# Latent attention's queries: channels on partitions for all tokens at once, in a step of three small parts

## Chip, cores and metric

The kernel runs on one core of one Trainium2 chip. The metric is the device time of one execution in microseconds, the median of the runs shown. TensorE (PE in the profile) does all matrix products and the transposes, VectorE (DVE), ScalarE (ACT) and GpSimd (POOL) do the elementwise work, and SyncE (SP) issues nearly all transfers.

## What is computed

Two layers of a network work on 384 tokens: 128 context tokens and 256 latent tokens. Each layer has a mixer of four attention branches (A to D) between one wide input projection and one output projection, and then an MLP. The change lies in branch A, latent attention. Cut to what matters (`wuq` is `mla_w_uq`, 256 x 384):

```python
q_lat, kv_lat, k_pe = h @ w_in            # 256, 128 and 32 columns
qa = (rmsnorm(q_lat, q_norm) @ wuq).reshape(b, t, 4, 96)
q_nope, q_pe = qa[..., :64], qa[..., 64:]  # 64 columns a head without position, 32 with
ckv = rmsnorm(kv_lat, kv_norm)             # also an output, with k_pe
q = concat(q_nope, rope(q_pe))             # rope on the 256 latent tokens only
k = concat(ckv @ w_uk, rope(k_pe) for every head);  v = ckv @ w_uv
o = softmax(q @ k.T * 96 ** -0.5) @ v
```

## The kernel before

The 384 tokens are three tiles of 128. Every large product is made in three passes of a split number (high x high, low x high, high x low): lines L122, L123 and L124, through a helper, so all large products of the program carry these lines. For the weights' halves ScalarE casts the high half (L283) and VectorE subtracts to get the low one (L127). A stream of weight blocks comes over SP's queue.

Inside a layer the program issues *ticks*. A tick is one group of 24 large matmuls (a token tile times eight channel blocks times three passes; 256 columns wide in the projections to the branches, 384 wide in the gates that follow) plus one step of a pipeline, `pipe`. The pipeline holds a list of tasks, each of them a row of stages; every step takes one new task in and runs one stage of every task that is under way. The order of the list is that of the `pipe.add` calls: branch A's preparation, A's attention, C's preparation and attention, D's, then branch B (whose last stages, `out_b`, end in the transposes L1096). A tick also issues some vector steps of a modulation (L378 on VectorE), whose number a tick is set by `TICK_OPS`: none in ticks 1 to 3, one a tick from tick 4, one every second tick from 14, two a tick from 29. Before ticks begin, layer 0 writes the condition's rows, `cond_rows`: four pieces, each a tanh on ScalarE (L233) and two operations on VectorE (L234, L235), into scratch tiles `acc` of the ring `t2`. That ring has ten tiles (`T2N`) and also holds the projections' results: `evac_to` (L644, on ScalarE) copies a PSUM bank out to a `t2` tile, which may have to wait until the tile's earlier user is done. Of the banks for the groups (pool `psg`) a group needs one, so a group has to wait for the copy of the bank that it takes over. A scheduler then orders the instructions of each engine within limits; the order that it makes is what the engines run, each its own from first to last.

Branch A before the change, for each token tile t, in three stages (`prep_a(t)`):

- `norms`: squares and sums on ScalarE (L790, L791), two steps on VectorE (L792, L794), the inverse root as a power on GpSimd (L190); two transposes of the 256 query latents (L799) and their copy (L800); the scaled key latents (L803).
- `up_q`: the product with `wq`, 128 tokens x 384 columns in two parts of 128 channels (L819; each product of full fp32 shows as two matmuls in the trace), transposes of the key latents and of the position key (L821, L822), a copy out on ScalarE that scales by the root (L824), and rotation (`rope`: two multiplications on GpSimd, L765 and L766, beside four operations on VectorE, L768, L771, L772).
- `turn`: four transposes, one a head (L837), and a copy to `qTA` (L838).

Then come `keys_a` (L845 to L847) and `values_a` (L854, L855), and the attention (L690 scores, L728 transposes of the weights, L746 product with the values).

Of the kernel before, what the change touches and what calls it, by code (L numbers as in the profile page):

```python
# [12 lines left out]
AF = mybir.ActivationFunctionType  # L13
ALU = mybir.AluOpType
AX = mybir.AxisListType

P = 128
D = 1024
KT = D // P
NTOK = 384  # L20
L = 2
D_FF = 4096
ALPHA = float((2.0 * L) ** 0.25)
EPS = 1e-6
# [71 lines left out]
def kernel(ctx, tc, a):  # L96
    nc = tc.nc
# [4 lines left out]
    psa = ctx.enter_context(tc.tile_pool(name="psa", bufs=3, space=bass.MemoryType.PSUM))  # L102
# [5 lines left out]
    mm = nc.tensor.matmul  # L108
# [6 lines left out]
    def bank(pool):  # L115
        return pool.tile([P, 512], F32, tag="bank", name=nm("bank"))
# [349 lines left out]
    for l in range(L):  # L466
        last = l == L - 1
        pipe = Pipe()
# [145 lines left out]
        def t2(name):  # L614
            return at.tile([P, 512], F32, tag="t2", name=nm(name), bufs=T2N)
# [163 lines left out]
        va = at.tile([P, 4, 256], F32, tag="va", name=nm("va"))  # L779
        rsa = at.tile([P, 3, 2], F32, tag="rsa", name=nm("rsa"))  # L780

        def prep_a(t):
            st_ = {}
            tok = slice(t * P, (t + 1) * P)
            rs = rsa[:, t]

            def norms():
                x = tm["a", t]
                sq = t2("sq")
                nc.scalar.activation(sq[:, 0:256], x[:, 0:256], AF.Square, accum_out=rs[:, 0:1])  # L790
                nc.scalar.activation(sq[:, 256:384], x[:, 256:384], AF.Square, accum_out=rs[:, 1:2])  # L791
                nc.vector.tensor_scalar(out=rs[:, 0:1], in0=rs[:, 0:1], scalar1=1.0 / 256, scalar2=EPS, op0=ALU.mult,  # L792
                                        op1=ALU.add)
                nc.vector.tensor_scalar(out=rs[:, 1:2], in0=rs[:, 1:2], scalar1=1.0 / 128, scalar2=EPS, op0=ALU.mult,  # L794
                                        op1=ALU.add)
                rsqrt(rs, rs, 2)
                tb = bank(psm)
                for k in range(2):
                    nc.tensor.transpose(tb[:, k * P:(k + 1) * P], x[:, k * P:(k + 1) * P], ident)  # L799
                nc.vector.tensor_copy(sq[:, 0:256], tb[:, 0:256])  # L800
                st_["qlT"] = sq
                kv = x[:, 256:384]
                nc.vector.scalar_tensor_tensor(out=kv, in0=kv, scalar=rs[:, 1:2], in1=rows[:, R_KV:R_KV + P],  # L803
                                               op0=ALU.mult, op1=ALU.mult)
                if t == 0:
                    nc.sync.dma_start(out=a["o_ckv"][0, l], in_=kv)
                    nc.sync.dma_start(out=a["o_kpe"][0, l], in_=x[:, 384:416])
                    st_["pe"] = x[:, 384:416]
                else:
                    r = small([P, 1, 2, 16], "kpe", 2)  # L810
                    rope(r, x[:, 384:416].rearrange("p (h s f) -> p h s f", h=1, s=2), cos_a[:, t - 1, 0:16],
                         sin_a[:, t - 1, 0:16], 16)()
                    st_["pe"] = r.rearrange("p h s f -> p (h s f)")

            def up_q():
                qlT = st_["qlT"]
                qb = bank(psa)
                for k in range(2):
                    mm(qb[:, :384], lhsT=qlT[:, k * P:(k + 1) * P], rhs=wq[:, k], start=(k == 0), stop=(k == 1))  # L819
                tb = bank(psm)  # L820
                nc.tensor.transpose(tb[:, 0:P], tm["a", t][:, 256:384], ident)  # L821
                nc.tensor.transpose(tb[:32, P:2 * P], st_["pe"], ident)  # L822
                q = t2("qA")
                nc.scalar.mul(q[:, :384], qb[:, :384], rs[:, 0:1])  # L824
                nc.vector.tensor_copy(ckvT[:, tok], tb[:, 0:P])
                nc.scalar.copy(kTA[64:96, :, tok], tb[0:32, P:2 * P].unsqueeze(1).to_broadcast([32, 4, P]))
                if t:
                    qv = q[:, :384].rearrange("p (h d) -> p h d", h=4)[:, :, 64:96].rearrange("p h (s f) -> p h s f", s=2)
                    rq = small([P, 4, 2, 16], "rqo", 1)
                    rope(rq, qv, cos_a[:, t - 1, 0:16], sin_a[:, t - 1, 0:16], 16)()  # L830
                    nc.vector.tensor_copy(qv, rq)
                st_["q"] = q

            def turn():
                tb = bank(psm)
                for h in range(4):
                    nc.tensor.transpose(tb[:96, h * P:(h + 1) * P], st_["q"][:, h * 96:(h + 1) * 96], ident)  # L837
                nc.scalar.copy(qTA[:96, :, tok], tb[:96].rearrange("p (h n) -> p h n", h=4))  # L838

            return norms, up_q, turn  # L840

        def keys_a():
            for i in range(2):
# [260 lines left out]


        for t in range(3):
            pipe.add(*prep_a(t))
        pipe.add(keys_a)
        pipe.add(values_a)
        ba, bc, bd = attend(0, lambda g, j, q: qTA[:96, 2 * g + j, q], lambda g, j, k: kTA[:96, 2 * g + j, k],  # L1110
                            lambda g, j, b: va[:, b, (2 * g + j) * 64:(2 * g + j + 1) * 64], MLA_SCALE), \
            attend_cd("c"), attend_cd("d")
# [510 lines left out]
def _pack(v):  # L1623
# [34 lines left out]
    rows[:, R_SINK:R_SINK + 4] = v["win_sink"][:, order]  # L1658
    out["rows"] = rows
    wm = np.zeros((L, P, 1280), f)  # L1660
    wm[:, :, 0:768] = v["mla_w_uq"].reshape(L, 2, P, 384).transpose(0, 2, 1, 3).reshape(L, P, 768)
    wm[:, :, 768:1024] = v["mla_w_uk"]
    wm[:, :, 1024:1280] = v["mla_w_uv"]
    out["wmla"] = wm
# [59 lines left out]
```

## Time and profile before

| | |
|---|---|
| median of 3 runs | 1275.6 us (1275.33 to 1277.57) |
| profiled execution | 1278.41 us, its span 1276.3 us |
| mean granted TensorE clock | 0.996 |
| busy: TensorE, its weight loads | 1255.7 us (98%), 1140.0 us (89%) |
| busy: VectorE, ScalarE, GpSimd | 852.7 us (67%), 583.5 us (46%), 214.5 us (17%) |
| DMA moved | 211.65 MB, mean 166 GB/s |

The span runs from the first to the last instruction of the core; the device time has some 2 us more around it. The end of a matmul is modelled, so that a wait in the profile's idle columns is shorter than the time lost between two issues. Line numbers are those of the kernel before, unless a sentence says that they are of the kernel after.

### The profile page before, as it was taken

Reading aid. Unit: us, or ns where it says so; the run is one execution under the profiler, and the core shown is the slowest. Engines: PE = TensorE matmul, PEld = TensorE weight load, DVE = VectorE, ACT = ScalarE, POOL = GpSimd, SP = SyncE. Lnnn points to the kernel's source line nnn. Section 1 sums busy time; section 2 is a strip of 40 time slices with the busy share of each in tenths; the row PEclk is TensorE's granted clock in tenths of the full one; section 3 lists DMA queues with packets and bytes.
Section 4 is the critical chain, followed back from the end, with each engine's and each line's share of the span. In section 5 each row is a group of like instructions: output and inputs, shape, how many; then the busy total and the mean of one; then the engine's idle time right before and its main releaser. Section 6 shows DMA issues by size and latency. Waiting matters only on the chain. (4 is left out here: it accounts for less than half of the span.)

```text
span 1276.3 us, 19137 instructions
## 1 busy us (share of the span) xinstructions
PE 1255.7 (98%) x7264; PEld 1140.0 (89%) x7264; DVE 852.7 (67%) x1537; ACT 583.5 (46%) x1054; POOL 214.5 (17%) x218
## 2 busy tenths in 40 slices
PE   9999999999999999999999999999999999999996
PEld 7889888999889999999898988999998999999995
DVE  4676965899679999443486876597456893333345
ACT  4654563333446444454365566233343744444451
POOL 0032200333232000000061210024221500000004
PEclk9999999999999999999999999999999999999998
DMA  9843323469626787454324422348344263334421
GB/s 371 335 153 118 124 87 104 145 207 348 203 84 233 264 275 272 160 166 136 116 84 147 157 92 83 120 151 326 118 149 161 102 216 132 125 123 158 168 71 50
DMA packets 65259, 211.65 MB, mean 166 GB/s; under 512 B 9296, under 2 KB 13840, under 8 KB 65040
## 3 DMA queue, kind: packets, MB, share of 16 engines
q1 hardware_dynamic: 62448, 201.88, 45.1%
q0 software_dynamic: 2432, 8.42, 1.9%
q8 instruction: 57, 0.93, 0.3%
q14 instruction: 34, 0.28, 0.1%
q10 hardware_dynamic: 288, 0.14, 0.0%
HBM read 206.28 MB, written 4.13 MB: 165 GB/s over the span
## 5 line engine op out<-in xcount | busy, mean ns | idle before, releaser
L127 DVE TENSOR_TENSOR wl<-raw,wh 128x1024 fp32r<-128x1024 f32 (+1 forms) x249 | 315.3, 1271 | 291.5 <-ACT wh L283 291.0
L283 ACT CAST wh<-raw 128x1024 fp32r<-128x1024 f32 x247 | 258.3, 1050 | 438.8 <-PE bank L123 285.8
L122 PE MATMUL bank<-hTh,wh 128*128 128x384 f32 x1040 | 351.4, 338 | 0.0
L124 PE MATMUL bank<-hTh,wl 128*128 128x384 f32 x1040 | 348.8, 336 | 0.6 <-DVE wl L127 0.6
L123 PE MATMUL bank<-hTl,wh 128*128 128x384 f32 x1040 | 348.4, 335 | 0.0
L122 PEld LDWEIGHTS bank<-hTh,wh 128*128 128x128 f32 x1040 | 195.3, 188 | 4.7 <-issue 1.9
L123 PEld LDWEIGHTS bank<-hTl,wh 128*128 128x128 f32 x1040 | 195.3, 188 | 3.1 <-issue 0.9
L124 PEld LDWEIGHTS bank<-hTh,wl 128*128 128x128 f32 x1040 | 195.2, 188 | 1.2 <-DVE wl L127 0.9
L123 PE MATMUL bank<-wl,uh 128*128 128x512 f32 (+1 forms) x376 | 146.5, 390 | 0.1
L124 PE MATMUL bank<-wh,ul 128*128 128x512 f32 (+1 forms) x376 | 146.3, 390 | 0.0
L122 PE MATMUL bank<-wh,uh 128*128 128x512 f32 (+1 forms) x376 | 145.7, 387 | 0.0
L378 DVE CUSTOM_DVE_ANT_0 acc<-raw,csr,bT 128x1024 bf16<-128x1024 f32 x80 | 105.0, 1327 | 1.7 <-POOL rope L766 0.9
L1193 POOL TENSOR_TENSOR tt<-tt,tt 128x384 f32<-128x384 f32 x48 | 65.5, 1384 | 207.7 <-DVE tt L1192 207.6
L378 DVE CUSTOM_DVE_ANT_0 acc<-lnc,csr,bT 128x1024 bf16<-128x1024 f32 x80 | 100.3, 1288 | 0.0
L124 PEld LDWEIGHTS bank<-wh,ul 128*128 128x128 f32 x376 | 70.4, 188 | 14.8 <-DVE ul L127 0.4
L123 PEld LDWEIGHTS bank<-wl,uh 128*128 128x128 f32 x376 | 70.6, 188 | 13.9 <-DVE wl L127 0.6
L122 PEld LDWEIGHTS bank<-wh,uh 128*128 128x128 f32 x376 | 70.7, 188 | 13.3
L122 PE MATMUL bank<-wh,hTh 128*128 128x256 f32 x240 | 71.7, 299 | 0.2 <-ACT tmc L644 0.2
L124 PE MATMUL bank<-wh,hTl 128*128 128x256 f32 x240 | 68.7, 286 | 0.0
L123 PE MATMUL bank<-wl,hTh 128*128 128x256 f32 x240 | 68.3, 285 | 0.0
L399 POOL DMA_DIRECT2D gd<-gs x4 | 2.4, 595 | 290.5 <-DMA raw<-in_w_u_dram 158.0
L710 ACT ACTIVATE p<-bank,neg 128x384 f32<-128x384 f32 (+1 forms) x72 | 35.9, 509 | 30.1 <-DVE neg L707 16.2
(280 smaller groups left out, 1857.8 us busy)
## 6 DMA issues: line engine op xcount, KB each, us to landing
raw<-in_w_g_dram SPq DMA_DIRECT2D x64, 512.0 KB, 3.5
raw<-in_w_d_dram SPq DMA_DIRECT2D x62, 512.0 KB, 3.5
raw<-in_w_u_dram SPq DMA_DIRECT2D x58, 512.0 KB, 3.6
raw<-in_w_av_dram SPq DMA_DIRECT2D x40, 512.0 KB, 3.7
lnc<-in_w_av_dram SPq DMA_DIRECT2D x40, 512.0 KB, 4.3
raw<-in_w_q_dram SPq DMA_DIRECT2D x28, 512.0 KB, 3.7
raw<-in_w_ada_dram SPq DMA_DIRECT2D x16, 512.0 KB, 8.4
raw<-in_w_b_dram SPq DMA_DIRECT2D x16, 512.0 KB, 3.5
```

The source lines that it names most:

```text
L122: mm(out, lhsT=a_hl[0], rhs=b_hl[0], start=start, stop=False)
L123: mm(out, lhsT=a_hl[0], rhs=b_hl[1], start=False, stop=False)
L124: mm(out, lhsT=a_hl[1], rhs=b_hl[0], start=False, stop=stop)
L127: nc.vector.tensor_tensor(out=low, in0=x, in1=high.bitcast(F32), op=ALU.subtract)
L283: nc.scalar.copy(wh, raw)
L378: nc.vector.tensor_tensor_reduce(out=alloc().bitcast(BF16), in0=w, in1=csr[:, c], scale=1.0, scalar=bT[:, l, u, b:b + 1], op0=ALU.mult, op ...
L399: nc.gpsimd.dma_start(out=g_dram[l][w].rearrange("c (k p) -> (c k) p", p=P), in_=gs)
L710: nc.scalar.activation(p[:, j, c], ss[j][:, c], AF.Exp, bias=neg[:, i, j:j + 1], scale=scale, accum_out=su[:, i, j:j + 1])
L1193: nc.gpsimd.tensor_tensor(out=acc[c], in0=acc[c], in1=t_, op=ALU.add)
```

## The change

`prep_a(t)` goes. In its place are `norms_a(t)`, three tasks of one stage (squares, root, and the query latents scaled by the root in place, on ScalarE, L795 after the change); `turn_q` (six transposes of the scaled latents into two banks, L815, copied out by L817 on VectorE and ScalarE); one task of two stages, first `rope_q` with `turn_kv`, then `turn_rope`; `nope_q`; and `keys_a` and `values_a` as one task. `nope_q` makes the queries without position directly with channels on partitions, for all 384 tokens: the weight is the stationary side and the turned latents move, four products of 384 columns (L852). `rope_q` makes the queries with position for three tiles in one bank, six products of 128 columns (L836), and rotates those of tiles 1 and 2; `turn_rope` turns them, one transpose a tile (L859). The columns of `wq` are put into the order that this needs, on the host, when the weights are packed.

```diff
--- before.py
+++ after.py
@@ -779,65 +779,87 @@
         va = at.tile([P, 4, 256], F32, tag="va", name=nm("va"))
         rsa = at.tile([P, 3, 2], F32, tag="rsa", name=nm("rsa"))
 
-        def prep_a(t):
...
+        pa = {}
+
+        def norms_a(t):
+
+            def f():
+                rs, x = rsa[:, t], tm["a", t]
+                sq = small([P, 256], "tanh", 1)
+                nc.scalar.activation(sq, x[:, 0:256], AF.Square, accum_out=rs[:, 0:1])
+                nc.scalar.activation(sq[:, 0:128], x[:, 256:384], AF.Square, accum_out=rs[:, 1:2])
+                for i, n in enumerate((256, 128)):
+                    nc.vector.tensor_scalar(out=rs[:, i:i + 1], in0=rs[:, i:i + 1], scalar1=1.0 / n, scalar2=EPS,
+                                            op0=ALU.mult, op1=ALU.add)
                 rsqrt(rs, rs, 2)
...
+                nc.scalar.mul(x[:, 0:256], x[:, 0:256], rs[:, 0:1])
                 kv = x[:, 256:384]
                 nc.vector.scalar_tensor_tensor(out=kv, in0=kv, scalar=rs[:, 1:2], in1=rows[:, R_KV:R_KV + P],
                                                op0=ALU.mult, op1=ALU.mult)
                 if t == 0:
                     nc.sync.dma_start(out=a["o_ckv"][0, l], in_=kv)
                     nc.sync.dma_start(out=a["o_kpe"][0, l], in_=x[:, 384:416])
...
+                    pa["pe", t] = x[:, 384:416]
                 else:
                     r = small([P, 1, 2, 16], "kpe", 2)
                     rope(r, x[:, 384:416].rearrange("p (h s f) -> p h s f", h=1, s=2), cos_a[:, t - 1, 0:16],
                          sin_a[:, t - 1, 0:16], 16)()
...
+                    pa["pe", t] = r.rearrange("p h s f -> p (h s f)")
+            return f
+
+        def turn_q():
+            pa["q"] = []
+            for k in range(2):
+                tb = bank(psm)
+                for t in range(3):
+                    nc.tensor.transpose(tb[:, t * P:(t + 1) * P], tm["a", t][:, k * P:(k + 1) * P], ident)
+                q = t2("qlT")[:, :NTOK]
+                (nc.scalar.copy if k else nc.vector.tensor_copy)(q, tb[:, :NTOK])
+                pa["q"].append(q)
+
+        def turn_kv():
+            tb = bank(psa)
+            for t in range(3):
+                nc.tensor.transpose(tb[:, t * P:(t + 1) * P], tm["a", t][:, 256:384], ident)
+            nc.vector.tensor_copy(ckvT[:, :NTOK], tb[:, :NTOK])
+            tb = bank(psa)
+            for t in range(3):
+                nc.tensor.transpose(tb[:32, t * P:(t + 1) * P], pa["pe", t], ident)
+            nc.scalar.copy(kTA[64:96, :, :NTOK], tb[0:32, :NTOK].unsqueeze(1).to_broadcast([32, 4, NTOK]))
+
+        def rope_q():
+
+            b = bank(psm)
+            for t in range(3):
+                tok = slice(t * P, (t + 1) * P)
                 for k in range(2):
...
+                    mm(b[:, tok], lhsT=pa["q"][k][:, tok], rhs=wq[:, k, 256:384], start=(k == 0), stop=(k == 1))
+            r = pa["r"] = t2("ropeq")
+            nc.vector.tensor_copy(r[:, :NTOK], b[:, :NTOK])
+            for t in (1, 2):
+                qv = r[:, t * P:(t + 1) * P].rearrange("p (h s f) -> p h s f", h=4, s=2)
+                if t == 1:
+                    rq = r[:, NTOK:].rearrange("p (h s f) -> p h s f", h=4, s=2)
+                else:
                     rq = small([P, 4, 2, 16], "rqo", 1)
...
+                rope(rq, qv, cos_a[:, t - 1, 0:16], sin_a[:, t - 1, 0:16], 16)()
+                pa["rq", t] = rq.rearrange("p h s f -> p (h s f)")
+
+        def nope_q():
+            for i in range(2):
+                b = bank(psa)
+                for k in range(2):
+                    mm(b[:, :NTOK], lhsT=wq[:, k, i * P:(i + 1) * P], rhs=pa["q"][k], start=(k == 0), stop=(k == 1))
+                nc.scalar.copy(qTA[0:64, 2 * i, :], b[0:64, :NTOK])
+                (nc.scalar.copy if i else nc.vector.tensor_copy)(qTA[0:64, 2 * i + 1, :], b[64:128, :NTOK])
+
+        def turn_rope():
+            tb = bank(psm)
+            for t in range(3):
+                nc.tensor.transpose(tb[:, t * P:(t + 1) * P], pa["rq", t] if t else pa["r"][:, 0:P], ident)
+            for h in range(4):
+                (nc.vector.tensor_copy if h == 0 else nc.scalar.copy)(qTA[64:96, h, :],
+                                                                      tb[32 * h:32 * h + 32, :NTOK])
 
         def keys_a():
             for i in range(2):
@@ -1104,9 +1126,11 @@
 
 
         for t in range(3):
-            pipe.add(*prep_a(t))
-        pipe.add(keys_a)
-        pipe.add(values_a)
+            pipe.add(norms_a(t))
+        pipe.add(turn_q)
+        pipe.add(lambda: (rope_q(), turn_kv()), turn_rope)
+        pipe.add(nope_q)
+        pipe.add(lambda: (keys_a(), values_a()))
         ba, bc, bd = attend(0, lambda g, j, q: qTA[:96, 2 * g + j, q], lambda g, j, k: kTA[:96, 2 * g + j, k],
                             lambda g, j, b: va[:, b, (2 * g + j) * 64:(2 * g + j + 1) * 64], MLA_SCALE), \
             attend_cd("c"), attend_cd("d")
@@ -1658,7 +1682,10 @@
     rows[:, R_SINK:R_SINK + 4] = v["win_sink"][:, order]
     out["rows"] = rows
     wm = np.zeros((L, P, 1280), f)
-    wm[:, :, 0:768] = v["mla_w_uq"].reshape(L, 2, P, 384).transpose(0, 2, 1, 3).reshape(L, P, 768)
+
+    uq = v["mla_w_uq"].reshape(L, 2, P, 4, 96)
+    uq = np.concatenate([uq[..., :64].reshape(L, 2, P, 256), uq[..., 64:].reshape(L, 2, P, 128)], -1)
+    wm[:, :, 0:768] = uq.transpose(0, 2, 1, 3).reshape(L, P, 768)
     wm[:, :, 768:1024] = v["mla_w_uk"]
     wm[:, :, 1024:1280] = v["mla_w_uv"]
     out["wmla"] = wm
```

Three places in the order of instructions. **ScalarE, start of layer 0's first ticks, before the change:** `tma` is the projection to A, `acc` is `cond_rows`' scratch, `tmd_676` is the copy of the first tick's group, `sq` squares.

```order
L644 COPY tma_620<-bank_249 128x416
L233 ACTIVATE acc_623<-csr 128x512
L233 ACTIVATE acc_627<-csr 128x512
L233 ACTIVATE acc_631<-csr 128x512
L233 ACTIVATE acc_635<-csr 128x512
L644 COPY tmd_676<-bank_651 128x256
L790 ACTIVATE sq_678,rsa_609<-tma_616 128x256
L791 ACTIVATE sq_678,rsa_609<-tma_616 128x128
```

After the change, at the same place:

```order
L644 COPY tma_620<-bank_249 128x416
L789 ACTIVATE tanh_678,rsa_609<-tma_616 128x256
L790 ACTIVATE tanh_678,rsa_609<-tma_616 128x128
L789 ACTIVATE tanh_715,rsa_609<-tma_618 128x256
L795 ACTIVATE tma_616<-tma_616,rsa_609 128x256
L790 ACTIVATE tanh_715,rsa_609<-tma_618 128x128
L795 ACTIVATE tma_618<-tma_618,rsa_609 128x256
L233 ACTIVATE acc_623<-csr 128x512
L233 ACTIVATE acc_627<-csr 128x512
L233 ACTIVATE acc_631<-csr 128x512
L233 ACTIVATE acc_635<-csr 128x512
L644 COPY tmd_676<-bank_651 128x256
```

The squares of tiles 0 and 1 and both scalings now stand ahead of the four tanh of `cond_rows`, and so ahead of the copy of the first group's bank.

**TensorE, between the second and the third group of 256 columns.** Before, between the first (`bank_651`) and the second group (`bank_691`), there were two transposes and nothing ahead of the third:

```order
L123 MATMUL bank_651<-wl_569,hTh 128x256
L124 MATMUL bank_651<-wh_568,hTl 128x256
L799 MATMUL bank_684<-ident,tma_616 128x128 x2
L122 MATMUL bank_691<-wh_564,hTh 128x256
L123 MATMUL bank_691<-wl_565,hTh 128x256
```

After, at the end of the second group (`bank_688`) and the start of the third (`bank_731`, which takes over the first group's PSUM and waits for the copy to `tmd_676`):

```order
L124 MATMUL bank_688<-wh_568,hTl 128x256
L815 MATMUL bank_812<-ident,tma_616 128x128
L815 MATMUL bank_812<-ident,tma_618 128x128
L815 MATMUL bank_818<-ident,tma_616 128x128
L815 MATMUL bank_818<-ident,tma_618 128x128
L122 MATMUL bank_731<-wh_564,hTh 128x256
L123 MATMUL bank_731<-wl_565,hTh 128x256
```

Four transposes of scaled latents (`tma_616` and `tma_618`, written by L795) now stand ahead of the third group.

**VectorE, the rotation of the queries, after the change.** `bank_858` is the bank of `rope_q`, `ropeq` its copy, `rqo` the rotated part of tile 2; TensorE's L859 turns them after 21 matmuls of the group in progress.

```order
L824 COPY ckvT_605<-bank_882 128x384
L838 COPY ropeq_865<-bank_858 128x384
L768 TENSOR_TENSOR ropeq_865<-ropeq_865,cst 128x4x16 x2
L771 TENSOR_TENSOR ropeq_865<-ropeq_865,rope_867 128x4x16
L772 TENSOR_TENSOR ropeq_865<-ropeq_865,rope_867 128x4x16
L768 TENSOR_TENSOR rqo_874<-ropeq_865,cst 128x4x16 x2
L771 TENSOR_TENSOR rqo_874<-rqo_874,rope_875 128x4x16
L772 TENSOR_TENSOR rqo_874<-rqo_874,rope_875 128x4x16
```

Before, each tile had its own copy and its own rotation, one tick apart. Now both rotations follow one another behind one copy, and the second writes into the same scratch of GpSimd (`rope`, one buffer) as the first. In TensorE's order everything that the pipeline issues behind branch A's preparation stands two ticks later than before (five tasks ahead of A's attention have become seven): branch C's first scores (L690) come after 18 groups instead of 16, and the three transposes of `out_b` (L1096) after 34, 35 and 36 groups instead of 32, 33 and 34. The number of ticks is the same.

## Rows read from the trace of the kernel before

**Rows 1.** The page's first part: busy time of each engine.

```profile
PE 1255.7 (98%) x7264; PEld 1140.0 (89%) x7264; DVE 852.7 (67%) x1537; ACT 583.5 (46%) x1054; POOL 214.5 (17%) x218
```

**Rows 2.** Windows: length, busy of PE, PEld, DVE, ACT, POOL; clock, DMA share, GB/s.

```profile
57.00:76.00 19.00, 18.45 (x117) 14.87 (x117) 12.94 (x36) 11.56 (x30) 6.36 (x11) 1.00 0.47 156
666.00:690.00 24.00, 23.70 (x156) 19.81 (x155) 14.09 (x36) 14.78 (x30) 5.60 (x14) 1.00 0.51 167
127.00:180.00 53.00, 51.36 (x339) 44.68 (x339) 45.97 (x130) 34.17 (x93) 8.29 (x7) 1.00 0.35 118
280.00:320.00 40.00, 40.00 (x232) 39.83 (x231) 39.58 (x55) 14.06 (x19) 12.81 (x11) 1.00 0.87 320
```

**Rows 3.** Timeline of TensorE, layer 0: start, us, instructions of latent attention.

```profile
58.74 1.46 PE L819 MATMUL bank<-wmla,sq 128*128 128x384 f32 x4
60.03 0.27 PE L821 MATMUL bank<-ident,tma 128*128 128x128 f32 x1
60.14 0.27 PE L822 MATMUL bank<-ident,tma 128*32 128x128 f32 x1
...
207.00 1.16 PE L990 MATMUL bank<-tmb,kd 128*128 128x128 f32 x8
208.08 0.71 PE L1009 MATMUL bank<-qkB 64*128 64x128 f32 x8
```

**Rows 4.** Timeline of TensorE: a wait inside latent attention, layer 0.

```profile
67.58 0.28 PE L123 MATMUL bank<-wl,hTh 128*128 128x256 f32 x1
68.30 0.91 PE L819 MATMUL bank<-wmla,sq 128*128 128x384 f32 x2 [0.44 <-DVE sq L800]
```

**Rows 5.** Timeline of ScalarE, 52 to 58 us.

```profile
52.87 1.70 ACT L233 ACTIVATE acc<-csr 128x512 f32<-128x512 f32 x3
...
56.08 0.38 ACT L644 COPY tmd<-bank 128x256 f32<-128x256 f32 x1 [0.69 <-DVE csr L235]
...
57.10 0.29 ACT L791 ACTIVATE sq<-tma 128x128 f32<-128x128 f32 x1
```

**Rows 6.** Timeline of VectorE, 53 to 59 us.

```profile
53.27 0.25 DVE L768 TENSOR_TENSOR kpe<-tma,cst 128x16 f32<-128x16 f32 x2
...
57.58 0.15 DVE L792 TENSOR_SCALAR rsa<-rsa 128x1 f32<-128x1 f32 x1
...
58.66 0.35 DVE L803 SCALAR_TENSOR_TENSOR tma<-tma,rsa,rows 128x128 f32<-128x128 f32 x1 [0.55 <-POOL rsa L190]
```

**Rows 7.** Timeline of TensorE: first matmul of the third token tile's group.

```profile
56.94 0.28 PE L122 MATMUL bank<-wh,hTh 128*128 128x256 f32 x1
```

**Rows 8.** Timeline of TensorE around the longest wait, 338 to 344 us.

```profile
337.66 0.40 PE L123 MATMUL bank<-wl,mh 128*128 128x512 f32 x1
337.89 0.40 PE L124 MATMUL bank<-wh,ml 128*128 128x512 f32 x1
340.68 0.80 PE L122 MATMUL bank<-wh,mh 128*128 128x512 f32 x1 [2.39 <-DVE tt L1192]
...
343.83 0.43 PE L123 MATMUL bank<-wl,mh 128*128 128x512 f32 x1
```

**Rows 9.** Timeline of VectorE: rotation of 64 columns, layer 0.

```profile
66.90 0.49 DVE L768 TENSOR_TENSOR rqo<-qA,cst 128x64 f32<-128x64 f32 x2 [0.24 <-ACT qA L824]
...
67.62 0.23 DVE L772 TENSOR_TENSOR rqo<-rqo,rope 128x64 f32<-128x64 f32 x1
```

**Rows 10.** Timeline of TensorE: two waits of branch C, layer 0.

```profile
131.33 1.09 PE L728 MATMUL bank<-ident,p 128*128 128x128 f32 x8 [0.76 <-ACT p L717]
...
154.77 0.66 PE L728 MATMUL bank<-ident,p 128*128 128x128 f32 x4 [0.50 <-ACT p L717]
```

**Rows 11.** Timeline of VectorE, then of TensorE: branch B's output, layer 0.

```profile
258.95 2.10 DVE L1086 TENSOR_SCALAR oB<-oB,mv,rsb 128x64 f32<-128x64 f32 x4
...
262.73 0.41 PE L1096 MATMUL bank<-ident,oB 128*128 128x128 f32 x2 [1.47 <-DVE oB L1088]
...
263.16 0.34 PE L124 MATMUL bank<-o,wl 128*128 128x384 f32 x1
```

More of the change, by code (lines that the diff above doesn't have):

```diff
@@ L780 @@
         rsa = at.tile([P, 3, 2], F32, tag="rsa", name=nm("rsa"))
-        def prep_a(t):
[L783 to L795, printed above, removed]
-                rsqrt(rs, rs, 2)
[L797 to L801, printed above, removed]
+        pa = {}
[8 more added lines that the diff above has]
+                                            op0=ALU.mult, op1=ALU.add)
+                rsqrt(rs, rs, 2)
+                nc.scalar.mul(x[:, 0:256], x[:, 0:256], rs[:, 0:1])
                 kv = x[:, 256:384]
@@ L807, in norms @@
                     nc.sync.dma_start(out=a["o_kpe"][0, l], in_=x[:, 384:416])
-                    st_["pe"] = x[:, 384:416]
+                    pa["pe", t] = x[:, 384:416]
                 else:
@@ L812, in norms @@
                          sin_a[:, t - 1, 0:16], 16)()
[L813 to L817, printed above, removed]
-                for k in range(2):
[L819 to L828, printed above, removed]
-                    rq = small([P, 4, 2, 16], "rqo", 1)
-                    rope(rq, qv, cos_a[:, t - 1, 0:16], sin_a[:, t - 1, 0:16], 16)()
-                    nc.vector.tensor_copy(qv, rq)
-                st_["q"] = q
@@ L834, in turn @@
[L834 to L840, printed above, removed]
+                    pa["pe", t] = r.rearrange("p h s f -> p (h s f)")
[9 more added lines that the diff above has]
+                pa["q"].append(q)
```

## Prediction, made before the changed kernel ran

> **What bounds the kernel now.** The first thing to read is the busy time [rows 1]: TensorE is busy 98% of the span, its weight loads 89%, VectorE 67%. The span therefore moves by two things only: work put on or taken off TensorE, and the few stretches where TensorE waits. The table of windows shows where these are [rows 2]: around branch A's preparation TensorE idles 0.55 us in layer 0 (57 to 76 us) and 0.30 us in layer 1 (666 to 690 us); around branch C in layer 0 it idles 1.64 us (127 to 180 us); from 280 to 320 us it never idles, but VectorE is busy 39.58 of 40 us there, so that it has almost nothing to spare. Work of ScalarE, VectorE and GpSimd that the change saves is worth nothing by itself; it counts only where TensorE waits for it. About 0.2% (2.55 us) is what a measurement of this kernel can tell from no change.
>
> **TensorE's own work.** Small fp32 instructions of branch A before [rows 3]: four of 384 columns take 1.29 us from their start to that of the next (58.74 to 60.03), 0.32 us each; a transpose takes 0.11 us (60.03 to 60.14). In a layer there are 24 transposes (2.6 us) and 12 of the former (3.9 us), together 6.5 us. After the change there are 15 transposes (1.65 us), the queries without position in four products, which are eight instructions of 384 columns (2.6 us), and the queries with position in six products, which are twelve instructions of 128 columns. The nearest row for these is L990, eight in 1.08 us (207.00 to 208.08), 0.135 us each: 1.6 us. Together 5.85 us, so 0.65 us a layer less, **-1.3 us** in all. At a transpose's 0.11 us, they would save 0.95 us a layer (-1.9 us); that is one end, -1.2 us the other.
>
> **Waits of the old chain.** `up_q` waits for the copy of the transposed latents: 0.44 us idle, and 0.72 us from the issue before it to its own [rows 4]. All idle time of the two stretches is 0.55 + 0.30 = 0.85 us [rows 2], and modelled ends hide part of each wait. I take **-1.5 us** for both layers, between -0.85 us and -1.9 us.
>
> **A new wait in layer 0.** This is the largest term. Before, ScalarE goes from the projections' copies straight to the four tanh of `cond_rows` at 52.87 us, and to the copy of the first group's bank at 56.08 us, which was held for 0.69 us by VectorE's product of the second piece [rows 5]. The third group, which takes over that bank, starts at 56.94 us [rows 7], half a microsecond after the copy's end: it just fits. After, the squares and scalings of tiles 0 and 1 stand ahead of the tanh, and each scaling waits for a root that goes over VectorE and GpSimd. From the first step on VectorE to the root's end this takes 1.08 us (57.58 to 58.66) [rows 6]. Worked out: VectorE must first finish the rotation of the position keys of both tiles (the second began at 53.27 us; a wide rotation takes 0.95 us from 66.90 to 67.85 [rows 9], this one is narrower: 0.8 us), 54.1 us; root of tile 0, 55.2; its scaling, as long as the 0.38 us copy of the same width, 55.6; the second square of tile 1 and the reading of its sum, 0.4 us (the square at 57.10 [rows 5] has VectorE's step at 57.58 [rows 6] behind it, 0.48 us at most), 56.0; root of tile 1, 57.1; its scaling, 57.5. The first tanh starts then, 4.6 us later than at 52.87, and the chain from it to the copy is unchanged: copy from 60.7 to 61.1 us. TensorE would come to the third group at 56.94 plus two more transposes, 57.2 us. It stands for 3.9 us, partly already at the transposes of tile 1's scaled latents. I take **+3.8 us**. The nearest zero is a copy that is not late at all; the upper end, with all rows a little longer, is 4.5 us. What is queued behind the copy (square and scaling of tile 2, the cast of the next weights) has two groups of time and is not late next.
>
> On this the Trainium skill (PSUM — Partial Sum Buffer, section Engine vs sequencer instructions) speaks against the change: ScalarE's queue is strictly first in, first out. By that rule the copy can't overtake the squares, and the sum is the one above; a queue that let a ready copy pass would take this term and the next out of it. No run here shows the two apart.
>
> **The clock after it.** After the longest wait of the kernel (2.39 us idle before 340.68) the next matmuls come slowly: from 340.68 to 343.83 seven matmuls of 512 columns, 0.45 us each, where two neighbours before the wait start 0.23 us apart (337.66 and 337.89) [rows 8]. That is 3.15 - 7 x 0.23, about 1.5 us, at twice the spacing: the lower of the clock's two levels (1.2 instead of 2.4 GHz). The wait before 262.73 us, 1.47 us idle, isn't followed by that: the matmul at 263.16 lasts 0.34 us for 384 columns [rows 11], as against 0.40 us for 512 before the long wait. A wait of 3.8 us, or of 3 us if the first part falls to the transposes, is nearer to the longer one: **+1.4 us**, between 0 and 1.5.
>
> The Trainium skill (TensorE: Matmul & The Clock Gate, Part 1: The HAM clock gate) says that the array falls to half its clock when it idles, comes back only after sustained activity, and that where this falls varies from run to run. By that rule the cost here could be nothing or a little more than the row's; the trace agrees with both kinds of wait.
>
> **The rotation.** `turn_rope` needs both rotations, which now follow one another through one scratch of GpSimd. A copy of 384 columns (0.5 us, by the 0.38 us for 256), then two rotations of 0.95 us [rows 9] and some 0.2 us of handing over make 2.6 us or a little more, and TensorE has 21 matmuls of 256 columns in between (half of the 0.23 us for 512 columns [rows 8], 0.12 us each: 2.5 us). **+1.0 us** for both layers as the two ends are 0 and 2, since each hand-over between three engines that is longer than I reckon shows in full. `rope_q` itself waits for two copies that stand behind transposes: **+0.2 us**.
>
> **Two ticks later.** What follows branch A's preparation moves by two groups. In layer 0 that puts most of C's attention under gate groups of 384 columns, 4.2 us a tick instead of 2.9 us (24 x 0.173 and 24 x 0.12, both by columns from the 0.23 us [rows 8]). C's transposes waited 0.76 and 0.50 us for the weights' sum on ScalarE [rows 10], and 1.64 us idle in all [rows 2]; longer ticks hide them partly: **-1.0 us**, between 0 and -2.2. Branch B's transposes waited 1.47 us for VectorE, which had four steps of 2.10 us in sum to do, and more behind them [rows 11]; they stand 8.3 us of TensorE time later now, but VectorE's work is also later, in the stretch where it has 0.42 us of 40 to spare [rows 2]: **-1.0 us**, between -1.5 and +2.1 (its step of 2.10 us shown in full as late weights). Layer 1 has the same moves with more slack: nothing, 0.8 us either way.
>
> **Sum.** -1.3 - 1.5 + 3.8 + 1.4 + 1.0 + 0.2 - 1.0 - 1.0 = +1.6 us. On the profiled execution, 1278.41 us, that is 1280.0; the median of the runs is 2.8 us below that execution, so the forecast is 1275.6 + 1.6 = **1277.2 us**.
>
> **Rivals.**
>
> 1. *VectorE falls behind in the gates of layer 0 (slower).* What comes two ticks later brings VectorE work into 280 to 320 us, and the weights' low halves are late by up to 2.1 us; B's wait then gives nothing back. 1277.2 + 1.0 + 2.1 = 1280.3 us. For it: 39.58 of 40 us. Against it: TensorE gets the moved steps there too, so time as well as work. It decides from about 0.5 us of uncovered VectorE work on.
> 2. *The third group doesn't wait (faster).* If roots come early or the copy is let through, +3.8 and +1.4 go: 1272.0 us. Against it: the order of ScalarE, and the 0.69 us that the copy already waited.
> 3. *The shift pays more, and the clock holds.* C's waits vanish (-1.2 more) and the clock doesn't fall (-1.4): 1274.6 us, no change that can be told.
>
> **Chances.** Forecast 0.5, rival 1 0.2, rival 2 0.15, rival 3 0.15. The bounds are 1273.05 and 1278.15 us. The forecast's own spread, 1275 to 1279.5 us, lies a third above the upper one: slower 0.17, same 0.32, faster 0.01. Rival 1 is slower but for 0.02, rival 2 faster but for 0.01, rival 3 same but for 0.04. In all faster 0.19, same 0.46, slower 0.35. The range runs from 1271.5 to 1281.0 us: it takes in rival 2 and rival 1, and leaves out about 2 in 10, where several bounds fall together.
>
> **What the profile after would show.** On ScalarE the first tanh near 57.5 us and the copy of the first group near 60.7; on TensorE an idle of about 3 us before the third group, at 61 us, with matmuls of doubled spacing behind it; L859's third transpose waiting for VectorE; no wait before the queries' products; less than 1.64 us idle around C; the three transposes of `out_b` without 1.47 us before them, and VectorE still nearly full to 320 us. I am wrong if the third group starts before 59 us, if the rotation costs more than 1 us a layer, or if weights come late between 270 and 325 us.

## The result, and the profile after

The changed kernel takes 1289.52 us (median of 4 runs, 1284.71 to 1291.11) against 1275.88 us of the kernel before beside it (4 runs): ratio 1.0104, 95% interval 1.0091 to 1.0117, 13.6 us slower. In a second measurement it took 1285.79 us (5 runs, 1284.22 to 1286.31) beside 1276.24 us: 1.0071, 1.0058 to 1.0084, 9.6 us slower. The profiled execution took 1291.11 us, its span is 1289.0 us, and the mean granted clock in it is 0.992.

The page's first part answers to [rows 1]. TensorE is busy 3.6 us longer, although it got less work, and its idle time grew by 9.1 us (29.7 against 20.6 us): it lost time by standing and by working more slowly.

```profile
PE 1259.3 (98%) x7262; PEld 1144.0 (89%) x7262; DVE 853.8 (66%) x1531; ACT 584.4 (45%) x1058; POOL 212.8 (17%) x218
```

The windows (length, busy of PE, PEld, DVE, ACT, POOL, clock, DMA share, GB/s). The first four answer to those of [rows 2], the third moved by the delay in it; the last three lie directly behind the three longest waits.

```profile
57.00:76.00 19.00, 15.73 (x107) 15.31 (x108) 10.09 (x21) 9.38 (x19) 0.80 (x2) 0.82 0.53 178
127.00:180.00 53.00, 50.97 (x340) 45.59 (x339) 45.26 (x109) 27.66 (x68) 15.78 (x15) 1.00 0.41 133
285.00:325.00 40.00, 39.42 (x228) 39.10 (x227) 40.00 (x51) 13.24 (x19) 14.04 (x12) 1.00 0.85 298
666.00:690.00 24.00, 21.91 (x160) 21.67 (x159) 14.48 (x26) 11.91 (x29) 10.36 (x10) 0.93 0.53 179
60.80:67.00 6.20, 6.18 (x29) 6.18 (x30) 2.81 (x7) 3.15 (x9) 0.69 (x1) 0.51 0.50 205
677.60:681.00 3.40, 3.31 (x16) 3.31 (x17) 0.66 (x3) 2.12 (x8) 0.69 (x1) 0.55 0.99 317
349.90:353.50 3.60, 3.56 (x9) 2.82 (x10) 3.60 (x4) 1.32 (x3) 2.95 (x2) 0.55 0.86 266
```

Read the second number of a row (TensorE) against the first, and the clock near the end: 57 to 76 us is idle for 3.27 us instead of 0.55, 127 to 180 us for 2.03 instead of 1.64, 285 to 325 us for 0.58 instead of nothing, 666 to 690 us for 2.09 instead of 0.30. In the last three stretches TensorE is busy, at about half its clock (0.51, 0.55 and 0.55). The first two are new; the third answers to the slow stretch that stood behind the longest wait before the change too [rows 8].

**Layer 0.** ScalarE, answering to [rows 5]:

```profile
55.01 0.51 ACT L795 ACTIVATE tma<-tma,rsa 128x256 f32<-128x256 f32 x1 [0.67 <-POOL rsa L190]
...
56.82 0.51 ACT L795 ACTIVATE tma<-tma,rsa 128x256 f32<-128x256 f32 x1 [1.00 <-POOL rsa L190]
57.23 1.65 ACT L233 ACTIVATE acc<-csr 128x512 f32<-128x512 f32 x3
...
60.39 0.37 ACT L644 COPY tmd<-bank 128x256 f32<-128x256 f32 x1 [0.70 <-DVE csr L235]
```

The two scalings end at 55.5 and 57.3 us, the first tanh starts at 57.23 (forecast 57.5), the copy of the first group's bank at 60.39 (forecast 60.7). TensorE at the same time, answering to [rows 4, 7]:

```profile
57.38 0.55 PE L815 MATMUL bank<-ident,tma 128*128 128x128 f32 x3 [0.42 <-ACT tma L795]
60.82 0.58 PE L122 MATMUL bank<-wh,hTh 128*128 128x256 f32 x1 [2.89 <-ACT tmd L644]
61.20 0.42 PE L123 MATMUL bank<-wl,hTh 128*128 128x256 f32 x1
61.41 0.41 PE L124 MATMUL bank<-wh,hTl 128*128 128x256 f32 x1
...
66.75 0.36 PE L122 MATMUL bank<-wh,hTh 128*128 128x256 f32 x1
66.95 0.28 PE L123 MATMUL bank<-wl,hTh 128*128 128x256 f32 x1
```

The transposes wait 0.42 us for the scaling and the third group 2.89 us for the copy. From 60.82 to 66.75 us 27 matmuls start, the first 0.38 and the others 0.21 us before the next; then the spacing is 0.12 us again. That is 5.93 - 27 x 0.12 = 2.7 us lost behind the wait.

**Layer 1**, where I had forecast nothing. TensorE, at the same step:

```profile
675.32 0.28 PE L124 MATMUL bank<-wh,hTl 128*128 128x256 f32 x1
677.69 0.42 PE L122 MATMUL bank<-wh,hTh 128*128 128x256 f32 x1 [2.09 <-ACT tmc L644]
677.92 0.41 PE L123 MATMUL bank<-wl,hTh 128*128 128x256 f32 x1
```

ScalarE there:

```profile
671.62 0.42 ACT L789 ACTIVATE tanh<-tma 128x256 f32<-128x256 f32 x1 [2.17 <-POOL x L1322]
...
675.08 0.51 ACT L795 ACTIVATE tma<-tma,rsa 128x256 f32<-128x256 f32 x1 [1.70 <-POOL rsa L190]
...
676.88 0.51 ACT L795 ACTIVATE tma<-tma,rsa 128x256 f32<-128x256 f32 x1 [1.00 <-POOL rsa L190]
677.29 0.35 ACT L644 COPY tmc<-bank 128x256 f32<-128x256 f32 x1
```

Again the copy of the first group's bank (677.29) stands behind the scalings of tiles 0 and 1, and they wait for the roots. The first square itself stood 2.17 us, until GpSimd's L1322 had ended. VectorE has four subtractions ahead of the first step of the root:

```profile
665.83 8.00 DVE L127 TENSOR_TENSOR wl<-raw,wh 128x1024 fp32r<-128x1024 f32 x4
673.75 0.14 DVE L792 TENSOR_SCALAR rsa<-rsa 128x1 f32<-128x1 f32 x1
```

Before the change the same four subtractions took the same 8.00 us (from 656.42 us), but there the copy of the bank stood ahead of the squares and waited for nothing but the group's last matmul:

```profile
663.35 0.37 ACT L644 COPY tmc<-bank 128x256 f32<-128x256 f32 x1 [2.35 <-PE bank L124]
```

**Later waits** (TensorE; the first two answering to [rows 10, 11]): branch C's transposes, branch B's, a late low half of weights, a gate's group that waits for a copy of ScalarE, the old longest wait [rows 8] in its new place, and branch B's transposes in layer 1.

```profile
171.72 0.55 PE L728 MATMUL bank<-ident,p 128*128 128x128 f32 x3 [1.05 <-ACT p L717]
...
281.27 0.41 PE L1118 MATMUL bank<-ident,oB 128*128 128x128 f32 x2 [0.74 <-DVE oB L1110]
...
293.22 0.44 PE L124 MATMUL bank<-hTh,wl 128*128 128x384 f32 x1 [0.58 <-DVE wl L127]
...
336.52 0.44 PE L122 MATMUL bank<-hTh,wh 128*128 128x384 f32 x1 [1.77 <-ACT tt L1189]
...
349.94 0.57 PE L122 MATMUL bank<-wh,mh 128*128 128x512 f32 x1 [2.03 <-DVE tt L1216]
...
880.69 0.41 PE L1118 MATMUL bank<-ident,oB 128*128 128x128 f32 x2 [1.45 <-DVE oB L1110]
```

C's transposes waited 0.50 us before and 1.05 now; B's 1.47 and 0.74; the waits of 0.58 and 1.77 us weren't there; the old longest one was 2.39 us and is 2.03. In layer 1 B's transposes wait 1.45 us, where they waited 0.34 (at 857.92 us).

**TensorE's own work** fell a little more than forecast. The twelve instructions of 128 columns take 1.36 us from the first start to that of the matmul behind them (1.60 with the modelled end of the last), so 0.11 us each and not 0.135; the eight of 384 columns, from 77.98 us, take 2.75 us with the end of the last, as forecast.

```profile
73.55 1.60 PE L836 MATMUL bank<-wmla,qlT 128*128 128x128 f32 x12
74.91 0.36 PE L122 MATMUL bank<-wh,hTh 128*128 128x256 f32 x1
```

### The profile page after: what moved, and what is told of

It is laid out like the page before. It is cut to its first block, busy times and chain, and to the rows that moved or that the text cites. A ratio compares the mean times of both kernels' runs of the same rounds, so it can differ in the third digit from the quotient of the medians.

```text
span 1289.0 us, 19114 instructions
## 1 busy us (share of the span) xinstructions
PE 1259.3 (98%) x7262; PEld 1144.0 (89%) x7262; DVE 853.8 (66%) x1531; ACT 584.4 (45%) x1058; POOL 212.8 (17%) x218
## 5 line engine op out<-in xcount | busy, mean ns | idle before, releaser
L122 PEld LDWEIGHTS bank<-wh,hTh 128*128 128x128 f32 x240 | 47.9, 199 | 8.2 <-ACT tmd L644 3.1
```

Of the source, the lines that this page charges most:

```text
L122: mm(out, lhsT=a_hl[0], rhs=b_hl[0], start=start, stop=False)
```

## The experiments

Theory 1: the squares float ahead of the copies on ScalarE, in both layers, and TensorE waits; behind a long wait its clock falls. Its rival, theory 2: the two ticks of shift are most of the loss. Each run stands beside the kernel before on its own chip: the one for layer 0 alone, the fillers, the first with all norms in front and the second measurement of the changed kernel on one (before: 1276.24 us), all others on another, on two occasions (before: 1275.64 and 1275.21 us).

**Where the squares write.** What lets them float stands in the diff: their scratch moved from the ring `t2` to a small buffer of its own. In layer 0 of the kernel before, the first square, behind the copy, started when VectorE had finished a piece of `cond_rows` (L235, the last step that reads the piece's scratch); that fits a slot of the ring coming free there:

```profile
56.69 0.42 ACT L790 ACTIVATE sq<-tma 128x256 f32<-128x256 f32 x1 [0.23 <-DVE csr L235]
```

The edit puts the scratch back:

```diff
-                sq = small([P, 256], "tanh", 1)
+                sq = t2("sq")[:, :256]
```

> Only the scratch of the squares goes back from a small buffer of its own to the ring t2, as in the kernel before; that puts the squares and scalings behind the copy of the first group's bank again, in both layers. Theory 1 (the order on ScalarE made two long waits, 3.7 us in layer 0 and 2.25 us in layer 1, and the clock fell behind each, 2.7 and 1.6 us): all 10.3 us of it go, 1279 us (1277.5 to 1281), and no matmul behind either place runs at doubled spacing. Theory 2 (the two ticks of shift are most of the loss): under 3 us of gain, about 1287 us. Theory 3 (scaling the latents on ScalarE costs, wherever it stands): the wait moves to the transposes L815, 1284 us or more.

1282.55 us (5 runs; before 1275.64; ratio 1.0052, 1.0038 to 1.0065). So 7.0 us less than the first measurement of the changed kernel and 3.2 us less than the second, which was made on another chip than this run; theory 1 had 10.3. The first square again waits 0.23 us for L235. Both waits for the copy are gone, but in layer 1 one has moved, as theory 3 has it, to the transposes of the scaled latents:

```profile
676.05 0.44 PE L815 MATMUL bank<-ident,tma 128*128 128x128 f32 x2 [2.01 <-ACT tma L795]
```

The same edit for layer 0 alone (`if l == 0`):

> The scratch of the squares goes back to the ring in layer 0 alone. Theory 1: layer 0's wait and the clock behind it go, up to 6.4 us: 1283.5 us (1282.5 to 1285); layer 1 keeps its 2.1 us wait, and what putting it back there gave is the rest of the 7.0 us, under 1 us, since there the wait moved to the transposes (2.01 us idle). If the layers share the gain evenly: 1286 us.

1282.34 us (6 runs; before 1276.24; 1.005, 1.0036 to 1.0065), beside the changed kernel's 1285.79 on the same chip: 3.4 us less. Putting layer 1's scratch back as well brought no more (3.2 us less than the same measurement, on another chip): in layer 1 it is a wait for a wait.

**The shift.** The changed kernel with five tasks, as before the change:

```diff
-        for t in range(3):
-            pipe.add(norms_a(t))
+        na = [norms_a(t) for t in range(3)]
+        pipe.add(na[0])
+        pipe.add(lambda: (na[1](), na[2]()))
         pipe.add(turn_q)
         pipe.add(lambda: (rope_q(), turn_kv()), turn_rope)
-        pipe.add(nope_q)
-        pipe.add(lambda: (keys_a(), values_a()))
+        pipe.add(lambda: (nope_q(), keys_a(), values_a()))
```

> The changed kernel with five tasks ahead of A's attention, as before the change (tiles 1 and 2 share one task of norms; queries without position, keys and values share one). The early squares stay. Theory 1: the two waits and their clock stay, only the price of the shift goes, which the trace leaves at some 6 us once the waits, the clock, the saved work (1.7) and the old waits (1.9) are taken off the 12.7: 1283.5 us (1281 to 1287). Theory 2: most of the loss goes, 1278 us or less.

1282.75 us (5 runs; 1.0053, 1.004 to 1.0065). Undoing the shift alone gives as much as undoing the early squares alone. Both together:

> Both edits together: scratch in the ring, five tasks. Theory 1: the waits (10.3 us) and the shift's price (6 us) both go; what is left is the saved work and the old waits, 1273 us (1271 to 1276), faster than the kernel before. If a merged task makes a new wait in its tick: 1276 to 1279 us.

1278.57 us (8 runs; 1.0024, 1.0014 to 1.0035). The shift is worth 4.0 us here (1282.55 to 1278.57) and the squares 4.2 (1282.75 to 1278.57), but the result is still slower than before, where theory 1 had it faster; it fits the other branch, new waits in merged tasks (the keys' products wait for a bank, 0.53 us at 76.27 and 1.09 us at 685.49 us). The edit that undoes the shift also merges tasks, so the 4.0 us are not the shift's alone. And the shift in the kernel before, by two empty tasks behind branch A's preparation:

```diff
         pipe.add(values_a)
+        for _ in range(2):
+            pipe.add(lambda: None)
```

> The kernel before with two empty tasks behind branch A's preparation, so that all that follows stands two ticks later and nothing else changes. If the shift costs what the trace leaves for it: 1282 us (1279 to 1284), with the waits of C, of the gates near 334 us and of out_b as in the changed kernel. If the shift pays, as the prediction had it: 1273.6 us. If it is free: 1275.9 us.

1279.9 us (5 runs; 1.0033, 1.002 to 1.0045): the shift costs 4.3 us by itself. Its waits on TensorE lie where those of the changed kernel lie, among them a late low half of weights (0.59 us at 287.71 us); the one before the gate's group is shorter, 0.80 instead of 1.77 us:

```profile
166.24 0.66 PE L728 MATMUL bank<-ident,p 128*128 128x128 f32 x4 [1.05 <-ACT p L717]
...
330.04 0.45 PE L122 MATMUL bank<-hTh,wh 128*128 128x384 f32 x1 [0.80 <-ACT tt L1167]
...
871.33 0.41 PE L1096 MATMUL bank<-ident,oB 128*128 128x128 f32 x2 [1.44 <-DVE oB L1088]
```

C's wait of 1.05 us (0.50 before) shows why longer ticks hide nothing. TensorE, first in the kernel before, then in this run:

```profile
152.81 0.92 PE L690 MATMUL bank<-qk 64*128 64x384 f32 x4
153.66 0.44 PE L122 MATMUL bank<-hTh,wh 128*128 128x384 f32 x1
153.94 0.33 PE L123 MATMUL bank<-hTl,wh 128*128 128x384 f32 x1
...
164.27 0.92 PE L690 MATMUL bank<-qk 64*128 64x384 f32 x4
```

The transposes start 1.96 us after the scores before (154.77 [rows 10]) and 1.97 us after them here (166.24), so the chain between them is as long as it was; on VectorE a modulation step of 1.27 us stands between the two small steps of the softmax's sum in both. But before, two matmuls of the group in progress stood between scores and transposes, and here none does: all of the chain behind the scores shows as idle time.

Then the other way, keys and values in one task of the kernel before:

```diff
-        pipe.add(keys_a)
-        pipe.add(values_a)
+        pipe.add(lambda: (keys_a(), values_a()))
```

> The kernel before with keys and values in one task, so that all behind branch A's preparation stands one tick earlier. Two ticks later cost 4.3 us. If the price runs with the distance, one tick earlier gains about 2 us: 1274 us. If the schedule of before is a good fit of steps to ticks by itself, any shift costs: 1277 us or more.

1279.76 us (5 runs; before 1275.21; 1.0037, 1.0025 to 1.005): 4.6 us slower. A shift isn't good or bad by its direction. The edit also puts two steps into one tick, but at that place the trace shows only 0.33 us idle (75.68 us), so most of the loss lies in what moved. The largest wait is in layer 1, branch C:

```profile
736.12 1.49 PE L728 MATMUL bank<-ident,p 128*128 128x128 f32 x8 [3.34 <-ACT p L717]
```

**The clock.** Seven small products that nobody reads fill the place where TensorE stood, between the second and the third group of layer 0:

```diff
             pipe.step()
             ticks[0] += 1
+            if l == 0 and not p2 and ticks[0] == 2:
+                fb = bank(psm)
+                for i in range(7):
+                    mm(fb[:, :256], lhsT=ident, rhs=tm["a", 1][:, 0:256], start=True, stop=True)
```

> The changed kernel with seven small fp32 products, whose result nobody reads, between the second and the third group of layer 0; they read tile 1's scaled latents, so they run where TensorE stood still, some 3.0 us long. Theory 1 (the clock fell because TensorE stood still): the third group still starts near 60.8 us, its matmuls start 0.12 us apart instead of 0.21, and the 2.7 us behind the wait go: about 1286.5 us, and the mean granted clock rises. Rival (the slow matmuls there have another cause, as contention or the transition between kinds): unchanged, 1289.5 us.

TensorE, the fillers and the start of the third group:

```profile
58.09 3.29 PE L479 MATMUL bank<-tma,ident 128*128 128x256 f32 x14 [0.55 <-ACT tma L799]
61.53 0.39 PE L122 MATMUL bank<-wh,hTh 128*128 128x256 f32 x1
```

The window behind it:

```profile
61.50:66.00 4.50, 4.47 (x37) 4.47 (x38) 2.55 (x7) 3.39 (x9) 0.70 (x1) 1.00 0.77 300
```

The group starts when it did (61.53 us; this execution started its first group later), and behind its first matmul the spacing is 0.12 us at once, at a clock of 1.00. That fits the standing as the cause at that place; it is one execution, and a full clock behind a wait also occurs without fillers (below). The time doesn't show it: 1285.41 us (6 runs, 1283.79 to 1288.3; 1.0073, 1.0058 to 1.0087) against 1285.79 of the changed kernel beside it:

> The changed kernel once more, as the standard for these and for its spread (1284.7 to 1291.1 us before, at a mean granted clock of 0.996 to 0.992). Theory 1: 1289 us, and run by run the time follows the clock: a fall of 0.004 in the mean clock goes with some 5 us.

Its five runs all had a clock of 0.996, and 1285.8 us; the first four had 0.992 (1291.11 us), 0.994 twice (1289.7 and 1289.34) and 0.996 (1284.71). Theory 1 had 1289 us for this one. So some 4 us of the 13.6 (1289.52 less 1285.79) go with the clock, and it doesn't fall as far in every execution. In this one's trace the two stretches behind the same two waits (2.90 and 2.11 us idle) read:

```profile
61.60:67.00 5.40, 5.36 (x32) 5.36 (x33) 2.83 (x7) 3.18 (x9) 0.70 (x1) 0.68 0.49 198
674.30:678.00 3.70, 3.69 (x30) 3.69 (x31) 0.81 (x4) 2.67 (x9) 0.70 (x1) 1.00 1.04 396
```

The clock is 0.68 behind the first and full behind the second. Behind the first, 17 matmuls lose 1.5 us, as against 2.7 us in the other trace; the 1.5 us that the other lost in layer 1 and the 1.6 us behind its wait at 349.94 us are not lost here: 4.3 us in all. In the profiled execution with the fillers the clock was low at these two other places (0.64 from 347.1 to 350.7 us and 0.63 from 674.7 to 678.7), and a spread of that size can hide what the fillers gained. What decides where the clock falls isn't shown.

**What is left of the change.** The scratch in the ring, five tasks, all norms in the first task, the second empty, keys ahead of the queries without position:

```diff
...
+        na = [norms_a(t) for t in range(3)]
+        pipe.add(lambda: [f() for f in na])
+        pipe.add(lambda: None)
         pipe.add(turn_q)
         pipe.add(lambda: (rope_q(), turn_kv()), turn_rope)
...
+        pipe.add(lambda: (keys_a(), nope_q(), values_a()))
```

> From the kernel with the scratch in the ring and five tasks: the norms of all three tiles in the first task, an empty second one, the turned latents in the third as there, and keys ahead of the queries without position in the last. If what it still lost to the kernel before (2.9 us) lies in the waits of the new chain (transposes for the scaled latents, 0.2 us in layer 0 and 1.2 in layer 1; key latents 0.69; the bank of the keys 0.53 and 1.09): those 3.7 us go, 1275 us (1273.5 to 1277). If the waits only move to the scaling of the third tile or to the copy of a group's bank: 1278 us or more.

1276.98 us (12 runs; before 1276.24; 1.0008, 1.0 to 1.0017), and a second time:

> The kernel with the scratch in the ring, five tasks and all norms first, once more, beside the spread one on one chip: 1277 us (1276 to 1278.5), no difference from the kernel before that can be told.

1277.55 us (11 runs; before 1275.21; 1.0017, 1.0008 to 1.0026). Beside it the same with the steps on PSUM spread over three tasks:

```diff
...
+        pipe.add(lambda: (turn_kv(), turn_q()))
+        pipe.add(lambda: (rope_q(), keys_a()), turn_rope)
+        pipe.add(lambda: (nope_q(), values_a()))
```

> As the kernel with all norms in the first task, but the steps that use PSUM are spread: key latents are turned with the query latents in the third task, the keys come with the queries with position in the fourth, queries without position with the values in the fifth. If the waits for a bank that the former still showed (0.35 us in layer 0, 1.08 in layer 1) and part of the one for the scaled latents (1.05 and 0.92) go: 1.5 to 2 us less, 1275 us, at or below the kernel before. If the wait for the scaled latents is all that counts: 1276.5 us or more.

1277.55 us (11 runs; 1.0014, 1.0005 to 1.0023): no better than the other, though steadier. Its waits in branch A, TensorE:

```profile
61.48 0.33 PE L823 MATMUL bank<-ident,tma 128*128 128x128 f32 x1 [1.11 <-DVE rsa L792]
...
63.28 0.33 PE L823 MATMUL bank<-ident,tma 128*128 128x128 f32 x1 [0.58 <-DVE tma L797]
...
667.49 0.33 PE L823 MATMUL bank<-ident,tma 128*128 128x128 f32 x1 [0.83 <-DVE tma L797]
...
682.50 1.13 PE L876 MATMUL bank<-wmla,ckvT 128*128 128x256 f32 x4 [1.02 <-DVE qTA L854]
```

They sum to 3.54 us idle, with a wait of 0.21 us at 76.61 to 3.75, against 0.85 us before [rows 2].

## Why the prediction was wrong

*TensorE's own work, -1.3 us:* right in kind, a little small. At 0.11 us for each of the twelve instructions a layer saves 0.9 us, so 1.9 us are saved, the low end of the range given.

*The new wait in layer 0, +3.8 us:* right in place, chain and size (0.42 + 2.89 us idle, and the modelled ends beyond it). The order of ScalarE was read; that the scratch made it was not.

*The clock, +1.4 us:* right in kind, too small: 2.7 us in the profiled execution and 1.5 us in the other trace of the changed kernel. I had capped it at 1.5 us with one row of a shorter wait [rows 8].

*Two ticks later, -1.0 - 1.0 us, and "layer 1 ... nothing":* these are the steps that failed. The shift costs 4.3 us by the kernel before with two empty tasks, where I had it give back 2.0. I argued from the ticks' length; but a wait lies between steps that stand close to one another in their engines' orders, and those move together. What changes is which matmuls, modulation steps and weight splits come between: C's transposes lost the two matmuls that had covered 0.55 us of their wait. A part of rival 1 came true (a late low half of weights, 0.58 us instead of 2.1), and with it one of the signs that I had named. The row had put C's wait down to ScalarE, whose scaling (L717) comes last; the sum ahead of it is finished on VectorE. In layer 1 I didn't look where ScalarE's copies had gone, and the wait of layer 0 stands there too: 2.09 us idle, and in the profiled execution 3.4 us at a clock of 0.55, 1.5 us more. Branch B's transposes wait 1.45 us there instead of 0.34, in the changed kernel and in the kernel before with two empty tasks alike (1.44).

*Waits of the old chain, -1.5 us:* they went, but new ones took their place. Before, the root was needed only by the copy out after the product (L824); now the latents are scaled before they are turned, and the root lies on TensorE's way. In the best arrangement tried this is 3.75 us idle against 0.85, so 2.9 us more, less the 1.9 us saved: 1.0 us, inside the measured interval (0.6 to 2.9 us). The rotation's +1.0 us I saw at most as 0.30 us idle, in the run with both edits; in the changed kernel neither it nor the +0.2 us for `rope_q`'s copies shows as a wait.

Together: the shift 4.0 us and the squares 4.2 us, each by undoing it beside the other, and the 2.9 us that are left with both undone (new chain less saved work) make 11.1 us, between the two measurements of 9.6 and 13.6 us. The rest of the larger one goes with the clock, as its runs' clocks say. Open is why the clock falls in one execution and not in another behind the same wait, and the waits between 336 and 350 us, whose place and length differ from run to run: 2.39 us at 340.68 before the change, 1.77 and 2.03 us at 336.52 and 349.94 after it, 0.66 us at 339.55 in the last run above. The profiled execution before, on which the forecast was built, was 2.8 us over the median; that this wait made it so isn't shown.

## What to carry to other kernels

A scratch tile's ring is also a place in the order: moving a scratch out of a contended ring let its writer float ahead of copies that TensorE needs, so look what each engine's order became in every layer, not only in the first. This pipeline lost 4.3 us by two ticks later and 4.6 us by one tick earlier, so a rewrite should keep the number of tasks, or be costed with empty tasks first. And a factor that is applied after a product is off its path; applied before, it is on it.

## What was not expected of the hardware

VectorE's four subtractions from 665.83 us take 8.00 us, after the change as before it. The first line gives their durations (shortest, median and longest in ns); below it are GpSimd's operations at the time:

```profile
L127 DVE TENSOR_TENSOR wl<-raw,wh x4: 1235/2316/2359, 665.8 to 672.6; 128x1024 fp32r<-128x1024 f32 x4
665.81 1.29 POOL L1322 TENSOR_TENSOR x<-x,lnc 128x512 f32<-128x512 f32 x1
667.07 2.28 POOL L1321 TENSOR_TENSOR x<-z,lnc 128x512 f32<-128x512 f32 x1
669.43 2.15 POOL L1322 TENSOR_TENSOR x<-x,lnc 128x512 f32<-128x512 f32 x1
671.67 1.08 POOL L765 TENSOR_TENSOR rope<-tma,cst 128x16 f32<-128x16 f32 x1
```

Three subtractions take 2.3 us and the last 1.24; the mean of all of this shape is 1.28 us. GpSimd's first operation, which started 0.02 us ahead of the first subtraction, takes its usual 1.29 us, the next two 2.28 and 2.15, and a multiplication of 16 columns 1.08 us that takes 0.23 us at 675.01. The ends alternate: GpSimd at 667.10, VectorE near 668.1 (its next subtraction starts at 668.12), GpSimd at 669.35, VectorE near 670.4, GpSimd at 671.58, VectorE near 672.6, GpSimd at 672.75. Each of the long operations ends 1.0 to 1.3 us behind the other engine's, about one undisturbed duration, and the short one 0.1 us behind it.

The Trainium skill (SBUF — State Buffer, section SBUF: two separate sides) says that VectorE and GpSimd share a pair of ports to SBUF by an exclusive lock, which a VectorE operation with two inputs in SBUF takes against a GpSimd operation that reads SBUF. The trace agrees, in that each operation stands until the other engine's is done and then runs at its usual length, and in that the subtractions at 664.40 us, which read one input from PSUM, ran at 0.69 us each beside a GpSimd operation of the usual 1.30 us (664.43).
